# Rotary factors made in one go, a gain row spread by TensorE, and another order of products in the last MLP pieces

## The chip, the cores and the metric

One core of one Trainium2 chip runs the whole program. Its engines work side by side: TensorE (PE) multiplies matrices and transposes, VectorE (DVE) and ScalarE (ACT) work on tiles, GpSimd (POOL) does small operations and issues some DMAs, SyncE (SP) issues the others. Each engine takes its instructions in order and waits on semaphores for the others. The metric is the device time of one execution in microseconds (us); lower is better. The kernel before took 1451.28 us, the median of 3 runs (1450.83 to 1451.67).

## The reference

A two-layer encoder on 512 positions of width 1024, all in float32. Each layer is a token mixer and an MLP, each behind an RMS norm with a gain:

```python
for i in range(DEPTH):
    h = rms_norm(x, norm_mix[i])
    ...
    y = dilated_mixer(h, ...) if i == 0 else mla_mixer(h, ...)
    x = x + y
    h = rms_norm(x, norm_ffn[i])
    x = x + sq_relu_mlp(h, ffn_w1[i], ffn_w2[i])
```

The first mixer projects h to queries, keys and values of three head groups (eight heads of 128 each). Queries and keys of group g get an RMS norm per head with a gain of that group (`a_q_gain[g]`, `a_k_gain[g]`) and a rotary embedding:

```python
def rope(x, seq_len):
    ...
    return (xf * cos + rot * sin).astype(x.dtype)
def sq_relu_mlp(h, w1, w2):
    a = jax.nn.relu(h @ w1)
    return (a * a) @ w2
```

with w1 of 1024 x 4096 and w2 of 4096 x 1024.

## The kernel before

**Products.** Every float32 operand is split into a high and a low part (`whi` by ACT, `wlo` by DVE for weights; L220 and L221 for activations), and each product is three matmuls: high by high, high by low, low by high. The tile framework's scheduler puts the instructions of each engine in an order and inserts the waits, so the order on an engine is not that of the source.

**The start.** The tokens lie in four tiles of 128 x 1024. `load_x` (L249) loads a tile in two halves, `gain_table` (L223) loads a gain row and repeats it on all 128 partitions in the same DMA (512 KB written for 1024 numbers), `load_w0` (L253) loads the first four weight tiles of 512 KB, in turn with the token tiles. `norm_tile` (L206) squares a tile on ACT (L136), takes the root with a small DVE operation (L128) and a POOL operation (L131), multiplies by the root and the gain on DVE (L212), transposes on PE (L123) into a PSUM bank `tp` (two banks in all) and splits into `hT` (ACT L220, DVE L221). Weights in the first block are all loaded before its products run; these products write four `acc` banks (L184).

**The rotary tables.** `tables(g)` (L281) loads the two gain rows of group g, again one DMA each that repeats the row on all partitions, and multiplies them into the cosine and sine constants: four DVE operations of 128 x 512 (L289, L291), giving `cosg[g]` and `sing[g]`. It is called for group g when that group's first query and key block is about to be evacuated: DVE multiplies each `acc` bank by these tables (L308, L311). Groups 1 and 2 take the DMA target from a buffer of the evacuation (`t1`).

**The pool of gain tables.** `gp` holds one buffer of 128 x 1024 under the tag `gain`. Whoever takes the tag next waits until all readers of the one before are done.

**The MLP.** It is cut into four pieces of 1024 columns. `up` makes the first product, `down` calls `wino` (L489), which forms the second product by seven products of half-sized blocks instead of eight. `ORDER` (L590) names them: the product's number, the chain of PSUM banks it adds into (`a` is the pair `sc`, `b` the pair `tp`, `d` the pair `tp` or, in the last piece, two `acc` banks), whether it begins the chain, and where its sum goes. Each is 24 matmuls of 512 columns. Its activation operand is a block of the activations (products 1, 2 and 4) or a sum or difference of blocks, made by DVE (L517); `split_a` (L483) splits it into `asp`. Its weights lie in four slots of `wqs`; products 6 and 4 need a sum of weight blocks, which is made by a DMA issued from POOL that adds into the slot (L509, 512 KB, two for each product). Such a DMA waits until the slot's earlier weights are split (L523, L524). After each product `put` (L551) adds its banks into `resid` (DVE L554); in the last piece (`done` is given) a finished row tile goes on to the next norm.

**Between the layers.** The second mixer's own tables, `cgB` and `sgB`, are made on POOL: eight products (L691, L692) and a sign change (L693), from gains `gr` that SP loads (L684) once the buffer they go to is free. POOL has one queue for these and for the DMAs of L509.

Of the kernel before, what the change touches and what calls it, by code (L numbers as in the profile page):

```python
# [17 lines left out]
P = 128  # L18
# [69 lines left out]
def encoder_kernel(ctx: ExitStack, tc: tile.TileContext, x, norm_mix, norm_ffn, a_w_qkv, a_q_gain, a_k_gain,  # L88
# [6 lines left out]
    def nm(s):  # L95
        uid[0] += 1
        return f"{s}_{uid[0]}"
# [143 lines left out]
    with tc.tile_pool(name="apool", bufs=1, reuse_waits="tile") as ap_, \  # L241
# [7 lines left out]
        def load_x(r):  # L249
            for hf in range(2):  # L250
                nc.sync.dma_start(xts[r][:, 512 * hf:512 * hf + 512], x_v[:, r, 512 * hf:512 * hf + 512])
# [2 lines left out]
            early[("first", k)] = load_raw(*qk_units(0, 0)[k], 512)  # L254
        cas = ap_.tile([P, 2176], F32, name="ca")
        ca = cas[:, 0:C_ALL - C_KEEP]
        load_x(0)
        gain_b = gain_table(norm_mix[0:1, :].rearrange("o d -> (o d)"), D, "g_mix0")
        nc.sync.dma_start(ck[:, 0:P], consts[:, 0:P])
        load_w0(0)  # L260
        load_x(1)
# [6 lines left out]
        nc.sync.dma_start(ck[:, P:C_KEEP], consts[:, P:C_KEEP])  # L268
        for r in range(NT):
            norm_tile(r, xts[r], gain_b, hT, aw, xn_tag="qkT")  # L270
        gqk0 = ap_.tile([P, 2, 512], F32, tag="gqk", name="gqk")

        def cc(a, b):
            return ca[:, a - C_KEEP:b - C_KEEP]
# [4 lines left out]
        sel, r4, sel2, i4 = cc(C_SEL, C_R4), cc(C_R4, C_SEL2), cc(C_SEL2, C_I4), cc(C_I4, C_ALL)  # L279

        def tables(g):  # L281

            gqk = gqk0 if g == 0 else aw.tile([P, 4, DH], F32, tag="t1", name=nm("gq"))
            for t, src in enumerate((a_q_gain, a_k_gain)):
                nc.sync.dma_start(gqk[:, t, 0:DH], src[0, g].partition_broadcast(P))
            for t in range(2):
                gb = gqk[:, t, 0:DH].rearrange("p (f d) -> p f d", f=2).unsqueeze(1)
                gb = gb.broadcast_to([P, NT, 2, 64])
                V.tensor_tensor(cosg[g][:, :, t].rearrange("p r (f d) -> p r f d", f=2),  # L289
                                cosA.unsqueeze(2).broadcast_to([P, NT, 2, 64]), gb, op=ALU.mult)  # L290
                V.tensor_tensor(sing[g][:, :, t].rearrange("p r (f d) -> p r f d", f=2), sinA, gb, op=ALU.mult)  # L291
# [197 lines left out]
    def wino(tag, Aq, w, wqs, pool, resid, done=None):  # L489
# [66 lines left out]
                    done(2 * i + t, n)  # L556

        banks = {}
        for p, chain, first, (i, n, op) in ORDER:
            a, wq = operands(p)  # L560
            at = split_a(a, pool)
            if first:
                pl, tg = {"a": (sc_p, "sc"), "b": (tp_p, "tp"), "d": (tp_p, "tp")}[chain]
                if done is not None and chain == "d":
                    pl, tg = acc_p, "acc"
                banks[chain] = [pl.tile([P, 512], F32, tag=tg, name=nm(tg)) for _ in range(2)]
            bk = banks[chain]

            tail = done is not None and p in (7, 4)
            parts = {}  # L570
            for u, t in ((0, 0), (1, 0), (0, 1), (1, 1)) if tail else ((0, 0), (0, 1), (1, 0), (1, 1)):
                if u not in parts:
                    parts[u] = split_w(wq[u])
                hi, lo = parts[u]
                for j in range(2):
                    k = 2 * u + j
                    ah = at[:, k, 0, t * P:(t + 1) * P]
                    al = at[:, k, 1, t * P:(t + 1) * P]
                    for i_, (lt, rt) in enumerate(((ah, hi), (ah, lo), (al, hi))):
                        PE.matmul(bk[t], lhsT=lt, rhs=rt[:, j], start=(first and k == 0 and i_ == 0),  # L580
                                  stop=(k == 3 and i_ == 2), skip_group_check=True)
            put(i, n, op, bk)
# [3 lines left out]
    for _ in range(3):  # L586
# [3 lines left out]
    ORDER = [(1, "a", True, (0, 0, ALU.add)), (5, "b", True, (1, 1, ALU.add)), (3, "b", False, (0, 1, ALU.add)),  # L590
             (6, "a", False, (0, 1, ALU.subtract)), (2, "d", True, (0, 0, ALU.add)),
             (7, "a", False, (1, 1, ALU.subtract)), (4, "a", False, (1, 0, ALU.add))]

    def mlp(layer, w1, w2, hT_m, resid, pool, done):
        a2s = {}
# [352 lines left out]
```

## Time and profile before

| | us |
|---|---|
| median of 3 runs | 1451.28 |
| the profiled execution | 1451.78 |
| its span on the core | 1449.6 |
| PE busy | 1410.4 |
| DVE busy | 887.1 |
| ACT busy | 727.2 |
| POOL busy | 198.4 |
| waits of PE for the first normalised tile | 8.9 |

The profile is one execution, taken by the hardware. A row of its timeline gives the start in us from the span's beginning, the duration in us, the engine, the line of the kernel, the operation, what is written from what (with partitions x elements), how many instructions the row holds, and in brackets the idle time ahead of it with what ended it. A row of the waits gives the engine, the tile and line that waited, what it waited for, the sum in us, how many times and the longest. A row of the windows gives a stretch, its length, the busy time of PE, its weight loads (PEld), DVE, ACT and POOL with the number of instructions, the granted TensorE clock as a share of full speed, the DMA share and GB/s.

### The profile page before, as it was taken

How to read it: one execution, taken by the hardware profiler on the slowest of the kernel's cores; microseconds unless marked ns; L12 is line 12 of the kernel's file. 1: busy time of each engine (PE TensorE's matmuls, PEld its weight loads, DVE VectorE, ACT ScalarE, POOL GpSimd, SP SyncE). 2: the span in 40 equal slices, each digit the busy share in tenths (PEclk: the TensorE clock that was granted, in tenths of full speed). 3: DMA queues.
4: the chain of work that ended last, by engine and by line, in shares of the span. 5: the costliest groups of instructions: out<-in, count | busy, mean ns of one | idle time of the engine just before them, and what ended most of it. 6: DMA issues, size and time to landing. Idle time of an engine off the chain costs nothing.

```text
span 1449.6 us, 19315 instructions
## 1 busy us (share of the span) xinstructions
PE 1410.4 (97%) x7116; PEld 1196.8 (83%) x7116; DVE 887.1 (61%) x1421; ACT 727.2 (50%) x1590; POOL 198.4 (14%) x197
## 2 busy tenths in 40 slices
PE   7999999999999999999999999899999999999998
PEld 6889889889988878888888877776768988888877
DVE  6765566566537655266475749788755266475647
ACT  5544455355335533453544545777633454544543
POOL 1120120011011101011020222332101011020210
PEclk9999999999999999999999999999999999999999
DMA  7325114321622344749394853310013749394853
GB/s 228 100 57 162 58 49 129 110 63 45 174 92 62 97 140 141 222 112 236 91 233 127 195 136 66 99 30 30 30 44 136 206 111 239 93 223 138 189 116 88
DMA packets 134813, 177.52 MB, mean 122 GB/s; under 512 B 8768, under 2 KB 73536, under 8 KB 134720
## 3 DMA queue, kind: packets, MB, share of 16 engines
q1 hardware_dynamic: 117312, 142.74, 31.1%
q0 software_dynamic: 17408, 33.56, 14.0%
q8 instruction: 56, 0.92, 0.2%
q14 instruction: 37, 0.30, 0.1%
HBM read 172.07 MB, written 4.19 MB: 122 GB/s over the span
## 4 chain that ended last, share of the span: by engine, by line
PE 89%; ACT 4%; DVE 3%; DMA 2%; issue 1%; POOL 1%; SPq 0%; DVEq 0%; ACTq 0%; POOLq 0%
PE acc L184 58%; PE sc L580 10%; PE tp L580 7%; PE tp L123 4%; PE acc L859 1%; PE acc L835 1%; PE sc L753 1%; PE sco L444 1%; PE sco L440 1%; PE sc L351 1%; PE sc L835 1%; ACT whi L157 1%; ACT junkb L136 1%; DVE wlo L158 1%; PE tp L859 0%
## 5 line engine op out<-in xcount | busy, mean ns | idle before, releaser
L184 PE MATMUL acc<-whi,hT 128*128 128x512 f32 (+2 forms) x1600 | 486.3, 379 | 5.6 <-DVE t L311 2.2
L158 DVE TENSOR_TENSOR wlo<-raw,whi 128x1024 fp32r<-128x1024 f32 (+3 forms) x170 | 195.7, 1156 | 230.5 <-ACT whi L157 229.5
L184 PEld LDWEIGHTS acc<-whi,hT 128*128 128x128 f32 x1600 | 296.2, 189 | 47.3 <-issue 2.9
L184 PE MATMUL acc<-hT_f,whi 128*128 128x512 f32 (+1 forms) x1152 | 319.4, 366 | 1.9 <-DVE resid L641 1.2
L157 ACT ACTIVATE whi<-raw 128x1024 fp32r<-128x1024 f32 (+3 forms) x170 | 170.0, 1005 | 269.0 <-PE acc L184 177.4
L184 PE MATMUL acc<-wlo,hT 128*128 128x512 f32 (+2 forms) x800 | 300.2, 375 | 0.2 <-DVE wlo L158 0.2
L184 PEld LDWEIGHTS acc<-hT_f,whi 128*128 128x128 f32 x1152 | 208.4, 189 | 37.8 <-DVE resid L641 1.6
L524 DVE TENSOR_TENSOR wlo<-wqs,whi 128x1024 fp32r<-128x1024 f32 x112 | 137.3, 1227 | 113.6 <-ACT whi L523 113.5
L184 PE MATMUL acc<-hT_f,wlo 128*128 128x512 f32 (+1 forms) x576 | 205.1, 365 | 0.0
L523 ACT ACTIVATE whi<-wqs 128x1024 fp32r<-128x1024 f32 x112 | 118.6, 1060 | 167.6 <-PE acc L184 66.2
L184 PEld LDWEIGHTS acc<-wlo,hT 128*128 128x128 f32 x800 | 151.2, 189 | 20.5 <-DVE wlo L158 1.1
L580 PE MATMUL sc<-whi,asp 128*128 128x512 f32 x512 | 165.1, 390 | 0.8 <-ACT asp L485 0.8
L509 POOL DMA_DIRECT2D wqs<-in_ffn_w_dram x64 | 77.6, 1350 | 528.4 <-DVE wlo L524 339.9
L184 PEld LDWEIGHTS acc<-hT_f,wlo 128*128 128x128 f32 x576 | 108.6, 189 | 17.5
L131 POOL TENSOR_TENSOR qrs<-rs_v,nhalf 128x4 f32<-128x4 f32 x48 | 61.5, 1290 | 408.3 <-DVE rs_v L128 393.8
L580 PE MATMUL tp<-whi,asp 128*128 128x512 f32 x352 | 112.2, 390 | 2.6 <-DVE asp L486 2.6
L580 PEld LDWEIGHTS sc<-whi,asp 128*128 128x128 f32 x512 | 96.1, 188 | 21.6 <-ACT asp L485 1.6
L580 PE MATMUL sc<-wlo,asp 128*128 128x512 f32 x256 | 99.6, 389 | 0.0
L580 PEld LDWEIGHTS tp<-whi,asp 128*128 128x128 f32 x352 | 65.9, 188 | 17.2 <-DVE asp L486 3.5
L580 PE MATMUL tp<-wlo,asp 128*128 128x512 f32 x176 | 68.5, 389 | 0.0
L136 ACT ACTIVATE junk<-acc 128x128 f32<-128x128 f32 x192 | 53.1, 277 | 18.9 <-PE acc L184 13.8
L554 DVE TENSOR_TENSOR resid<-resid,sc 128x512 f32<-128x512 f32 x64 | 43.0, 682 | 24.4 <-PE sc L580 24.4
(190 smaller groups left out, 1796.3 us busy)
## 6 DMA issues: line engine op xcount, KB each, us to landing
wqs<-in_ffn_w_dram SPq DMA_DIRECT2D x80, 512.0 KB, 5.1
raw<-in_ffn_w_dram SPq DMA_DIRECT2D x64, 512.0 KB, 4.4
wqs<-in_ffn_w_dram POOLq DMA_DIRECT2D x64, 512.0 KB, 7.2
raw<-in_a_w_qkv_dram SPq DMA_DIRECT2D x96, 256.0 KB, 3.4
raw<-in_a_w_qkv_dram SPq DMA_DIRECT2D x64, 192.0 KB, 2.8
raw<-in_a_w_o_dram SPq DMA_DIRECT2D x8, 512.0 KB, 4.0
raw<-in_b_w_o_dram SPq DMA_DIRECT2D x8, 512.0 KB, 3.7
xt<-in_x_dram SPq DMA_DIRECT2D x8, 256.0 KB, 5.7
```

What stands on the lines that cost most here:

```text
L123: PE.transpose(o, i, ident)
L131: G.tensor_tensor(out, v[:, :n], nhalf[:, :n], op=ALU.pow)
L136: A.activation(junk, x, AF.Square, scale=1.0 / math.sqrt(dim), accum_out=out)
L157: A.activation(hi[:, :nk, :n], raw[:, :nk, :n], AF.Copy)
L158: V.tensor_tensor(lo[:, :nk, :n], raw[:, :nk, :n], hi[:, :nk, :n].bitcast(F32), op=ALU.subtract)
L184: PE.matmul(accs[o][:, oc], lhsT=lt, rhs=rt, start=(kt == 0 and p_i == 0 and hv == 0), stop=(kt == total - 1 and p_i == 2), skip_group_che ...
L509: nc.gpsimd.dma_start(t, src, accum_op=ALU.add)
L523: A.activation(hi, x, AF.Copy)
L524: V.tensor_tensor(lo, x, hi.bitcast(F32), op=ALU.subtract)
L554: V.tensor_tensor(sl, sl, banks[t], op=op)
L580: PE.matmul(bk[t], lhsT=lt, rhs=rt[:, j], start=(first and k == 0 and i_ == 0), stop=(k == 3 and i_ == 2), skip_group_check=True)
L835: PE.matmul(sc, lhsT=lt, rhs=rt, start=(i == 0), stop=(i == 4))
```

## The change

Three parts. First, the gain row of the first norm is loaded as one row of 4 KB, ahead of the tokens, and spread over the partitions by two PE products of a column of ones with it; ACT copies the two PSUM banks into the gain buffer. Second, the gain rows of all three groups are loaded at once, behind the first norms, into the buffer of the tag `gain` (so they wait for the last reader of the first norm's gain, and the next norm's gain waits for the last table), and `tables(g)` loads nothing. Third, the last piece of each MLP runs its products in the order 1, 2, 5, 3, 6, 7, 4 instead of 1, 5, 3, 6, 2, 7, 4.

```diff
+        gain_b = gp.tile([P, D], F32, tag="gain", name="g_mix0")
+        ones = ap_.tile([1, P], F32, tag="P10", name="ones")
+        V.memset(ones, 1.0)
+        row = ap_.tile([1, D], F32, tag="P01", name="g_row")
+        nc.sync.dma_start(row, norm_mix[0:1, :])
         load_x(0)
-        gain_b = gain_table(norm_mix[0:1, :].rearrange("o d -> (o d)"), D, "g_mix0")
+        for hf in range(2):
+            tp = tp_p.tile([P, 512], F32, tag="tp", name=nm("tpg"))
+            PE.matmul(tp, lhsT=ones, rhs=row[:, 512 * hf:512 * hf + 512], start=True, stop=True)
+            A.activation(gain_b[:, 512 * hf:512 * hf + 512], tp, AF.Copy)
         nc.sync.dma_start(ck[:, 0:P], consts[:, 0:P])
...
-        gqk0 = ap_.tile([P, 2, 512], F32, tag="gqk", name="gqk")
+        gqks = gp.tile([P, D], F32, tag="gain", name="gqk")[:, 0:2 * NG * DH].rearrange("p (g t d) -> p g t d", g=NG, t=2)
+        for g in range(NG):
+            for t, src in enumerate((a_q_gain, a_k_gain)):
+                nc.sync.dma_start(gqks[:, g, t], src[0, g].partition_broadcast(P))
...
         def tables(g):
-
-            gqk = gqk0 if g == 0 else aw.tile([P, 4, DH], F32, tag="t1", name=nm("gq"))
-            for t, src in enumerate((a_q_gain, a_k_gain)):
-                nc.sync.dma_start(gqk[:, t, 0:DH], src[0, g].partition_broadcast(P))
+            gqk = gqks[:, g]
...
-        for p, chain, first, (i, n, op) in ORDER:
+        for p, chain, first, (i, n, op) in ORDER if done is None else ORDER_LAST:
...
+    ORDER_LAST = [ORDER[0], ORDER[4]] + ORDER[1:4] + ORDER[5:]
```

The lines behind the first part move by 9 to 12, so L289 and L291 become L298 and L300, L308 and L311 become L317 and L320, L509 becomes L518, L580 becomes L589, L691 to L693 become L703 to L705.

The scheduler moves more than the diff shows. On DVE, behind the last normalisation of the first norm (`xn` of the fourth tile), there stood before, with tp numbered by its use (`tp_190` and `tp_197` of the third tile, `tp_212` and `tp_219` of the fourth):

```order
L212 SCALAR_TENSOR_TENSOR xn_205<-xt_113,nrs_209,g_mix_6_117 128x1024
L221 TENSOR_TENSOR hT_91<-tp_190,hT_91 128x4x128
L158 TENSOR_TENSOR wlo_263<-raw_259,whi_262 128x1024
L221 TENSOR_TENSOR hT_91<-tp_197,hT_91 128x4x128
L289 TENSOR_TENSOR cosg_104<-ca,gqk 128x4x128
L291 TENSOR_TENSOR sing_107<-ca,gqk 128x4x128
...
L221 TENSOR_TENSOR hT_91<-tp_212,hT_91 128x4x128
L221 TENSOR_TENSOR hT_91<-tp_219,hT_91 128x4x128
L308 TENSOR_TENSOR t_59_296<-acc_243,cosg_104 128x512
```

In the changed kernel (`tp_199` and `tp_206` are of the third tile, `tp_221` of the fourth; `cosg_105`, `cosg_106` are of groups 1 and 2) there stands:

```order
L212 SCALAR_TENSOR_TENSOR xn_214<-xt_113,nrs_218,g_mix_115 128x1024
L221 TENSOR_TENSOR hT_91<-tp_199,hT_91 128x4x128
L298 TENSOR_TENSOR cosg_104<-ca,gqk 128x4x128
L300 TENSOR_TENSOR sing_107<-ca,gqk 128x4x128
...
L300 TENSOR_TENSOR sing_108<-ca,gqk 128x4x128
L221 TENSOR_TENSOR hT_91<-tp_206,hT_91 128x4x128
L298 TENSOR_TENSOR cosg_106<-ca,gqk 128x4x128
L300 TENSOR_TENSOR sing_109<-ca,gqk 128x4x128
L317 TENSOR_TENSOR t_60_309<-acc_256,cosg_104 128x512
...
L221 TENSOR_TENSOR hT_91<-tp_221,hT_91 128x4x128
```

Eight table operations, for groups 0 and 1, now stand ahead of the low half of the third tile's second transposes, and four more, with an evacuation, ahead of the fourth tile's.

On ACT, in the first norm of the changed kernel, the second copy of the gain row (`tpg_125`) stands behind the first weight split, and the square of the fourth tile (`xn_214`) behind the fourth weight split (`whi_275`), which it stood ahead of before:

```order
L267 ACTIVATE g_mix_115<-tpg_122 128x512
L157 ACTIVATE whi_260<-raw_129 128x1024
L267 ACTIVATE g_mix_115<-tpg_125 128x512
...
L157 ACTIVATE whi_275<-raw_272 128x1024
L220 ACTIVATE hT_91<-tp_184 128x4x128
L136 ACTIVATE xn_214,nss_213<-xt_113 128x1024
```

The square of the fourth tile now waits for the landing of the fourth weights, since ACT takes its rows in order.

On POOL, at the end of the first MLP, the second layer's tables stood between the accumulating DMAs before; the last of the 29 in the first row is product 6's first, the row behind L692 its second:

```order
L509 DMA wqs_5335<-in_ffn_w_dram 128x2x512 x29
L691 TENSOR_TENSOR cgB<-ck,gr 128x4x32
L692 TENSOR_TENSOR sgB<-ck,gr 128x4x32
...
L509 DMA wqs_5335<-in_ffn_w_dram 128x2x512
L693 TENSOR_SCALAR sgB<-sgB 128x8x32
```

In the changed kernel all table operations stand ahead of product 6's two DMAs and product 4's two, the four of the last row:

```order
L518 DMA wqs_5342<-in_ffn_w_dram 128x2x512 x28
L703 TENSOR_TENSOR cgB<-ck,gr 128x4x32
L704 TENSOR_TENSOR sgB<-ck,gr 128x4x32
...
L705 TENSOR_SCALAR sgB<-sgB 128x8x32
L518 DMA wqs_5342<-in_ffn_w_dram 128x2x512 x4
```

Product 6's first DMA moved behind all nine table operations. On PE, two matmuls of product 6 (into `sc`) stand ahead of product 3's 24 (into `tp`, the operand `asp_7502`) in that piece, behind product 5 (`asp_7460`):

```order
L589 MATMUL tp_7464<-wlo_7482,asp_7460 128x512
L589 MATMUL tp_7464<-whi_7481,asp_7460 128x512
L589 MATMUL sc_7381<-whi_7544,asp_7541 128x512
L589 MATMUL sc_7382<-whi_7544,asp_7541 128x512
L589 MATMUL tp_7463<-whi_7505,asp_7502 128x512
```

Product 3 had two matmuls of product 6 ahead of it before too, when both came a product earlier; behind the first MLP's last piece the order on PE is that of before again, until the last piece of the second MLP, which is reordered in the same way.

More of the change, by code (lines that the diff above doesn't have):

```diff
@@ L281, in tables @@
         def tables(g):
-            gqk = gqk0 if g == 0 else aw.tile([P, 4, DH], F32, tag="t1", name=nm("gq"))
-            for t, src in enumerate((a_q_gain, a_k_gain)):
-                nc.sync.dma_start(gqk[:, t, 0:DH], src[0, g].partition_broadcast(P))
+            gqk = gqks[:, g]
             for t in range(2):
-                gb = gqk[:, t, 0:DH].rearrange("p (f d) -> p f d", f=2).unsqueeze(1)
+                gb = gqk[:, t].rearrange("p (f d) -> p f d", f=2).unsqueeze(1)
                 gb = gb.broadcast_to([P, NT, 2, 64])
```

## The prediction

> **What bounds the kernel now.** I read the page first, then what TensorE (PE) waited for, then the three stretches that the change touches.
>
> ```profile
> span 1449.6 us, 19315 instructions
> PE 1410.4 (97%) x7116; PEld 1196.8 (83%) x7116; DVE 887.1 (61%) x1421; ACT 727.2 (50%) x1590; POOL 198.4 (14%) x197
> ```
>
> ```profile
> PE tp L580 <- DVE asp L486: 2.6, 2, 1.5
> ...
> PE acc L184 <- DVE t L311: 2.2, 1, 2.2
> ...
> PE sc L580 <- ACT asp L485: 0.8, 2, 0.4
> ```
>
> PE is busy 97% of the span, so 1449.6 - 1410.4 = 39 us is all that can be won by waiting less. The last three rows (us in total, times, longest) are what the change aims at: 2.2 us in front of the rotary evacuation L311, 2.6 + 0.8 us in the second MLP products. The number of products is unchanged, so the whole question is which waits go and which come. Matmuls of 512 columns follow each other every 0.227 us, from the rows of the last MLP piece below: 24 of them from 860.05 to 865.49 are 5.44 us.
>
> **The change, part 1: the start and the rotary tables.** The rows are in order of time; the last column is the idle time before and its releaser.
>
> ```profile
> 4.51 1.06 ACT L136 ACTIVATE xn<-xt 128x1024 f32<-128x1024 f32 x1 [2.28 <-DMA xt<-in_x_dram]
> 7.53 1.29 DVE L212 SCALAR_TENSOR_TENSOR xn<-xt,nrs,g_mix 128x1024 f32<-128x1024 f32 x1 [1.68 <-DMA g_mix<-in_norm_mix_dram]
> 9.38 1.06 ACT L157 ACTIVATE whi<-raw 128x1024 fp32r<-128x1024 f32 x1 [3.72 <-DMA raw<-in_a_w_qkv_dram]
> 10.47 1.23 DVE L158 TENSOR_TENSOR wlo<-raw,whi 128x1024 fp32r<-128x1024 f32 x1 [1.65 <-ACT whi L157]
> 10.97 0.79 PE L184 MATMUL acc<-whi,hT 128*128 128x512 f32 x1
> 20.53 1.28 DVE L212 SCALAR_TENSOR_TENSOR xn<-xt,nrs,g_mix 128x1024 f32<-128x1024 f32 x1 [0.66 <-POOL nrs L131]
> 21.02 1.06 ACT L157 ACTIVATE whi<-raw 128x1024 fp32r<-128x1024 f32 x1 [0.37 <-DMA raw<-in_a_w_qkv_dram]
> 21.88 0.34 SPq L285 DMA_DIRECT2D gqk<-in_a_q_gain_dram  x1
> 26.39 0.69 DVE L289 TENSOR_TENSOR cosg<-ca,gqk 128x512 f32<-128x512 f32 x1 [1.82 <-DMA gqk<-in_a_q_gain_dram]
> 26.99 0.68 DVE L291 TENSOR_TENSOR sing<-ca,gqk 128x512 f32<-128x512 f32 x1
> 38.31 0.84 PE L184 MATMUL acc<-whi,hT 128*128 128x512 f32 x3
> ```
>
> Without the 512 KB broadcast all later loads land sooner. It held the first normalisation 1.68 us, and landed 3.0 us behind the first tile (4.51 to 7.53); I take 2.3 us, between the two. The spreading matmuls run while PE has nothing to do (its first instruction before stands at 8.87) and cost nothing by themselves. But ScalarE's second copy of the gain now stands behind the first weight split (1.06), and VectorE's first normalisation behind wlo (1.23): weights at 7.0, split to 8.1, wlo to 9.3, and from the normalisation's start to the first product 3.4 before (7.53 to 10.97), less the 0.5 in which ScalarE was then busy with the split: 12.2, over 1 us late. This does not add up with what follows, since a later chain takes over.
>
> That chain: ScalarE's fourth weight split now stands ahead of the fourth tile's square. Weights at 21.0 - 2.3 = 18.7, split 1.06, copy 0.6, square with its accumulator 1.25, the small operations and pow 0.9, normalisation 1.28: 23.8, against 20.53 + 1.28 = 21.81. The gain DMAs wait for it, since they use the buffer that it reads. They land 3.4 us after issue by the later gains' row (next part), 4.4 by the first group's (21.88 to 26.29, just before 26.39). The queue carries less then, so I take 3.4: tables start at T0 = 27.3. VectorE now does eight table operations, 0.60 apart (26.39, 26.99), before the low-half copy L221 for which PE's next transposes wait, and four more before that of the fourth tile: 8 x 0.60 + 0.60 (L221) + 1.2 (two tables) + 0.7 (L317 and a small one) + 1.2 (two tables) + 0.7 (L320) + 0.6 (L221) = 9.8, so 37.1. From the matmul that waits there, 22 more stand ahead of the first of the next block: 37.1 + 22 x 0.227 = 42.1. Before, that matmul was the second of the three in the row at 38.31, at 38.54. **Start: +3.6 us.** Bounds: 2.5 (the loads 1 us earlier still) and 4.6 (gains land in 4.4). Behind the gain DMAs on SP stand g_ffn, which waits for the last table, and the next weights; these need a buffer that the next block's first split frees, and that split stands behind the tables on VectorE, so the SP queue is not what they wait for.
>
> **Part 2: what the early tables give back.**
>
> ```profile
> DMA to landing us min/median/max: 3.4/3.7/3.9
> ```
>
> ```profile
> 88.02 0.69 DVE L289 TENSOR_TENSOR cosg<-ca,gq 128x512 f32<-128x512 f32 x1 [6.66 <-DMA gq<-in_a_q_gain_dram]
> 93.67 0.41 PE L184 MATMUL acc<-whi,hT 128*128 128x384 f32 x1 [2.24 <-DVE t L311]
> ```
>
> ```profile
> 95.02:98.44 3.42, 3.42 (x13) 3.42 (x12) 3.42 (x7) 1.08 (x5) 1.37 (x1) 0.50 0.61 171
> ...
> 523.60:525.80 2.20, 0.11 (x2) 0.05 (x1) 2.20 (x4) 1.06 (x1) 0.00 (x0) 1.00 0.01 4
> ```
>
> VectorE sat 6.66 us for the third group's gains, and PE then waited 2.24 us for the evacuations behind four tables. In the windows (length, busy time of PE, PEld, DVE, ACT, POOL, then the granted clock) 3.42 us at clock 0.50 follow: half of it, 1.71 us, is lost. With the tables made early both go, and what is late next, the weight splits at that place, had its data in time: **-3.95 us** (-2.2 if the slow stretch comes from elsewhere). Parts 1 and 2 together: **-0.3 us**.
>
> **Part 3: the last piece of the first MLP.**
>
> ```profile
> 860.05 0.39 PE L580 MATMUL sc<-whi,asp 128*128 128x512 f32 x1
> ...
> 865.49 0.39 PE L580 MATMUL tp<-whi,asp 128*128 128x512 f32 x1
> ...
> 868.06 0.73 PE L580 MATMUL tp<-whi,asp 128*128 128x512 f32 x2 [1.50 <-DVE asp L486]
> ```
>
> ```profile
> PE tp L123 <- DVE xn L212: 1.0, 1, 1.0
> ```
>
> ```profile
> 866.47 0.45 POOL L691 TENSOR_TENSOR cgB<-ck,gr 128x128 f32<-128x128 f32 x1
> ...
> 871.50 1.44 POOL L692 TENSOR_TENSOR sgB<-ck,gr 128x128 f32<-128x128 f32 x1
> ...
> 873.68 1.55 POOL L693 TENSOR_SCALAR sgB<-sgB 128x256 f32<-128x256 f32 x1
> ```
>
> ```profile
> 870.21 1.06 ACT L523 ACTIVATE whi<-wqs 128x1024 fp32r<-128x1024 f32 x1 [3.45 <-PE tp L580]
> ```
>
> ```profile
> DMA to landing us min/median/max: 6.2/6.4/7.9
> ```
>
> Product 2 takes its operand straight from the activations, so it needs none of the sums that product 5 waited for: the 1.50 us go, and with product 6 later also its 0.43. The next layer's norm can start a product earlier, which removes the 1.01 us at its first transposes (the row of that stretch's waits). Sum **-2.94 us** (0 at worst, were all of them to come back in another place).
>
> The price stands on POOL. Before, the first accumulating DMA of product 6 was issued ahead of the eight table operations of the second layer; now it stands behind all eight and L693. These wait for the gains gr, whose buffer the last matmuls ahead of product 1 free in both kernels; so they end at 871.50 + 1.44 + 1.55 = 874.5. The DMA lands 6.2 later (the quickest of four), at 880.7, and its split is done at 881.7. PE has 72 matmuls ahead (products 1, 2, 5): 860.05 + 72 x 0.227 = 876.4. Its next two are product 6's, and product 3's 24 stand behind them: **a stall of 5.4 us**. Bounds: 1.4 if four more tables take 0.45 like the third instead of 1.44; 7.1 if the landing takes 7.9. A stall of 2.24 us was followed by a slow stretch, so one of 5.4 should be too: **+1.7 us** (0 to 3.4). Part 3 is -2.94 + 5.4 + 1.7 = **+4.2 us**.
>
> By the Trainium skill, "TensorE: Matmul & The Clock Gate", "Why this matters for your kernels", only gaps of more than about 3 us between bursts cost the clock. By it the slow stretch after 2.24 us would not be owed to that gap, the sum of part 2 would be -2.2, and the new gap would still cost its 1.7, 1456.5 in all. The trace has a drop behind 2.24 us and none behind the gap in the window at 523.60, and the measurement decides. The Trainium skill, "DMA: Bandwidth & Descriptors", "Anatomy of one DMA — SWDGE (gpsimd) path", prices a POOL transfer at 2.0 us plus bytes over 436 GB/s, an estimate of 3.2 us for 512 KB; by it the stall would be 2.4. The trace's 6.2 to 7.9 are nearly twice that and stand.
>
> **Part 4: the last piece of the second MLP.**
>
> ```profile
> 1409.92 1.22 DVE L524 TENSOR_TENSOR wlo<-wqs,whi 128x1024 fp32r<-128x1024 f32 x1
> ...
> 1412.92 0.73 PE L580 MATMUL tp<-whi,asp 128*128 128x512 f32 x2 [1.14 <-DVE asp L486]
> ```
>
> No tables stand on POOL here. The same reorder removes 1.14 + 0.33 (what is left of the totals 2.6 and 0.8). Product 3's first matmuls then stand behind product 6's and wait for a VectorE difference in their turn; nothing shows its size, between 0 and about 1.1 (the wait of the same kind just removed); I take 1.0, since VectorE does the same work in the same time. Product 6's first DMA adds into the buffer that product 5's split has read, and product 5 is now third: its first wlo takes the place of the row at 1409.92, done at 1411.1. The DMA lands by 1417.3 to 1419.0, its split is done by 1420.1, 1.7 us or more ahead of PE: PE had done 28 of the 72 matmuls at 1411.8, where the 1.14 us began, and 44 more take it to 1421.8. (In the first MLP the same distance from the piece's start is near 866, ahead of POOL's 874.5.) **-0.4 us.**
>
> **Sum.** -0.3 + 4.2 - 0.4 = +3.5 us. The profiled execution took 1451.78 us (span 1449.6 and 2.2 around it), 0.5 above the median of the runs; the difference carries over: 1451.28 + 3.5 = **1454.8 us**.
>
> **The rivals.** (a) The stall comes but the clock holds, or POOL's tables run faster: part 3 is then +2.5 or less, the sum +1.8, 1453.1. For it: gaps of 2 us left the clock at 1.00; against it: 5.4 is far longer. (b) On the other side: POOL gives no stall. The DMA then must land by 876.4 - 1.06 = 875.3, so be issued by 869.1, 5.4 us ahead of my 874.5. This needs the nine POOL operations in 5 us instead of 10.5, as if all took the 0.45 that one or two did. Then only the gains are left: -0.3 - 2.9 - 0.4 = -3.6, 1447.7: faster. (c) The early tables cost more: two stalls of some 1.5 us near 33 and 37 us, close together, cost the clock there (+1.7), or the gains land in 4.4 (+1.0): 1455.8 to 1457.5. (d) The change does not do what it says, the wait at 91 us staying in another form: part 2 falls short by up to 3.95, 1458.7; against it, nothing there reads gains any more. (e) The slow stretch at 95 us is not owed to the gap ahead of it and stays: part 2 is -2.2, 1456.5; for it speaks the gap at 523.60 that cost no clock, against it that nothing else stood still there. This is what the Trainium skill's rule on the clock, cited above, would make of it.
>
> **Chances.** Forecast 43%, (a) 26%, (b) 12%, (c) 12%, (d) 3%, (e) 4%. A measurement of this kernel can tell about 0.2%, 2.9 us, from no change: below 1448.4 is faster, above 1454.2 slower. (b) gives faster 0.12; (a) and the lower third of the forecast's spread give the same, 0.40; the rest slower, 0.48. The range leaves out (b), (d) and the end of (c): 1450.0 to 1457.6.
>
> **What would show it.** In the profile after: a PE wait of about 5 us on the split L523's data near 876 us, with POOL's table rows ahead of the first accumulating DMA, and a window at clock 0.50 behind it; no gap near 91 us, no drop at 95; the first matmul of the second block near 42 us. If POOL issues that DMA before 869, or the wait near 876 is missing, part 3 is wrong and with it the sign.

## The result, and the profile after

| | before | changed |
|---|---|---|
| median of 5 runs on one chip | 1450.83 us (1449.58 to 1451.67) | 1458.44 us (1457.45 to 1459.02) |
| ratio, 95% interval | | 1.0052 (1.0038 to 1.0067) |
| profiled execution | 1451.78 us, span 1449.6, mean granted clock 0.999 | 1458.44 us, span 1456.2, clock 0.994 |

The kernel became 7.6 us slower. On a second chip the changed kernel took 1457.78 us beside 1451.74, ratio 1.0044 (1.0031 to 1.0056): 6.0 us. The forecast was +3.5 us: the side was right, the size about half. Three executions were disturbed and stand outside the medians and ranges given below: the profiled one of the kernel that keeps PE busy (3676.68 us, so no row of it is shown), one of the kernel with one load for two groups (1860.83) and one of the kernel before (2252.59).

The first lines of the page of the changed kernel, the span, and each engine's busy time with its count of instructions:

```profile
span 1456.2 us, 19315 instructions
...
PE 1417.7 (97%) x7120; PEld 1202.4 (83%) x7120; DVE 886.0 (61%) x1422; ACT 729.1 (50%) x1592; POOL 201.3 (14%) x197
```

PE's idle time is what it was (1456.2 - 1417.7 = 38.5 us, 39.2 before), and PE is busy 7.3 us longer. Of these, 3.74 us are the four instructions that spread the gain row, in time in which PE only waited before. From its first transposes on (at 8.87 us before, at 12.16 now) the same 7116 instructions took 1414.0 us instead of 1410.4, with 30.0 us of idle time instead of 30.2: the waits that went and those that came cancel there, and the rest is matmuls that ran slower in some stretches, as the granted clock says too. So two questions have to be kept apart: where PE waits, and where its clock drops.

What PE waited for in three stretches of the changed kernel (us in total, times, longest): 12 to 130 us, the last piece of the first MLP, and that of the second:

```profile
PE tp L123 <- DVE rs_v L128: 6.0, 1, 6.0
PE acc L184 <- DVE hT L221: 1.4, 1, 1.4
PE tp L123 <- DVE hT L221: 1.0, 2, 0.6
...
PE sc L589 <- ACT whi L532: 4.4, 1, 4.4
...
PE tp L589 <- DVE resid L563: 0.9, 1, 0.9
```

The first row is the wait for the first normalised tile, which ends at 12.16 us. No wait is left near 91 us, and none of the three old ones in the first MLP; a wait of 4.4 us on a weight split stands there instead. In the second MLP 1.47 us became 0.9.

The start, rows in order of time (start, length, then the idle time before it and its releaser):

```profile
2.38 3.74 PE L266 MATMUL tpg<-g_row,ones 1*128 1x512 f32 x4 [2.38 <-DMA g_row<-in_norm_mix_dram]
...
8.60 1.06 ACT L157 ACTIVATE whi<-raw 128x1024 fp32r<-128x1024 f32 x1 [1.94 <-DMA raw<-in_a_w_qkv_dram]
...
11.39 1.06 ACT L157 ACTIVATE whi<-raw 128x1024 fp32r<-128x1024 f32 x1 [0.22 <-DMA raw<-in_a_w_qkv_dram]
...
13.31 0.60 ACT L220 ACTIVATE hT<-tp 128x512 fp32r<-128x512 f32 x1 [0.86 <-PE tp L123]
...
13.96 0.80 PE L184 MATMUL acc<-whi,hT 128*128 128x512 f32 x1
...
20.15 1.06 ACT L157 ACTIVATE whi<-raw 128x1024 fp32r<-128x1024 f32 x1 [2.84 <-DMA raw<-in_a_w_qkv_dram]
...
23.79 1.28 DVE L212 SCALAR_TENSOR_TENSOR xn<-xt,nrs,g_mix 128x1024 f32<-128x1024 f32 x1 [0.66 <-POOL nrs L131]
...
25.10 0.34 SPq L283 DMA_DIRECT2D gqk<-in_a_q_gain_dram  x1
...
28.58 0.69 DVE L298 TENSOR_TENSOR cosg<-ca,gqk 128x512 f32<-128x512 f32 x1 [2.91 <-DMA gqk<-in_a_q_gain_dram]
...
37.75 0.68 DVE L221 TENSOR_TENSOR hT<-tp,hT 128x512 fp32r<-128x512 f32 x1
38.48 0.74 PE L184 MATMUL acc<-whi,hT 128*128 128x512 f32 x2 [1.36 <-DVE hT L221]
...
43.40 0.84 PE L184 MATMUL acc<-whi,hT 128*128 128x512 f32 x3
```

The first product of the second block is the second matmul of the last row: about 43.6 us, where 38.54 stood before.

POOL in the last piece of the first MLP, and the split and product that wait for its transfer:

```profile
865.66 0.64 POOL L703 TENSOR_TENSOR cgB<-ck,gr 128x128 f32<-128x128 f32 x1 [26.44 <-DMA gr<-in_b_q_gain_dram]
...
874.25 1.71 POOL L705 TENSOR_SCALAR sgB<-sgB 128x256 f32<-128x256 f32 x1
875.92 2.50 POOL L518 DMA_DIRECT2D wqs<-in_ffn_w_dram  x2
...
882.26 1.06 ACT L532 ACTIVATE whi<-wqs 128x1024 fp32r<-128x1024 f32 x1 [4.98 <-DMA wqs<-in_ffn_w_dram]
883.37 1.22 PE L589 MATMUL sc<-whi,asp 128*128 128x512 f32 x2 [4.37 <-ACT whi L532]
```

Windows of 3.41 us of the changed kernel (busy time of PE, PEld, DVE, ACT, POOL; then granted clock, DMA share, GB/s), each drop with the window ahead of it:

```profile
523.52:526.93 3.41, 1.32 (x11) 1.01 (x10) 3.39 (x4) 1.06 (x1) 0.00 (x0) 1.00 0.19 73
526.93:530.34 3.41, 3.41 (x18) 3.41 (x17) 1.30 (x2) 1.19 (x2) 0.00 (x0) 0.50 0.31 60
878.51:881.92 3.41, 0.49 (x3) 0.07 (x1) 3.26 (x4) 0.00 (x0) 0.00 (x0) 1.00 1.07 178
881.92:885.33 3.41, 1.96 (x5) 1.58 (x6) 1.98 (x3) 1.39 (x2) 0.46 (x1) 0.50 0.70 128
885.33:888.75 3.42, 3.42 (x10) 2.65 (x9) 2.11 (x2) 2.73 (x3) 1.42 (x2) 0.50 0.51 63
...
939.95:943.36 3.41, 1.40 (x10) 1.35 (x10) 2.20 (x10) 3.38 (x18) 1.94 (x4) 1.00 0.16 66
943.36:946.77 3.41, 3.41 (x14) 2.75 (x13) 2.58 (x12) 3.12 (x13) 2.34 (x4) 0.50 0.02 5
1117.44:1120.85 3.41, 1.58 (x12) 1.18 (x11) 3.13 (x6) 1.46 (x4) 0.20 (x1) 1.00 0.94 336
1120.85:1124.26 3.41, 3.41 (x19) 3.41 (x18) 2.34 (x3) 1.47 (x2) 0.34 (x1) 0.50 1.01 354
```

Five windows at clock 0.50, where the profile before had one, at 95.02. Two follow the new wait near 882 us; the other three, at 527, 943 and 1121 us, lie where the change touches nothing.

Setting the matmuls of the two profiles side by side, one by one, shows where the 6.6 us of span arise. How much later the changed kernel's PE is:

| behind | later by |
|---|---|
| first product of the second block (before: 38.5 us) | 5.1 us |
| the old wait at 91 us and its slow window (before: 130 us) | a steady 0.85 |
| the slow window at 527 us | 2.47 |
| the last piece of the first MLP | 6.3, then 5.7 |
| the slow windows at 943 and 1121 us | 6.15, 7.13 |
| the last piece of the second MLP | 6.64 |

### The profile page after: what moved, and what is told of

Read it like the earlier page. It is cut to its first block, busy times and chain, and to the rows that moved or that the text cites. A ratio compares the mean times of both kernels' runs of the same rounds, so it can differ in the third digit from the quotient of the medians.

```text
span 1456.2 us, 19315 instructions
## 1 busy us (share of the span) xinstructions
PE 1417.7 (97%) x7120; PEld 1202.4 (83%) x7120; DVE 886.0 (61%) x1422; ACT 729.1 (50%) x1592; POOL 201.3 (14%) x197
## 4 chain that ended last, share of the span: by engine, by line
PE 86%; issue 3%; DVE 3%; ACT 3%; DMA 3%; POOL 1%; SPq 0%; ACTq 0%; POOLq 0%; DVEq 0%
PE acc L184 55%; PE sc L589 10%; PE tp L589 7%; PE tp L123 4%; PE acc L871 1%; DMA raw<-in_a_w_qkv_dram 1%; PE sc L765 1%; DMA wqs<-in_ffn_w_dram 1%; PE acc L847 1%; PE sco L449 1%; PE sco L453 1%; PE sc L360 1%; DVE wlo L158 1%; PE sc L847 1%; ACT junkb L136 1%
## 5 line engine op out<-in xcount | busy, mean ns | idle before, releaser
L532 ACT ACTIVATE whi<-wqs 128x1024 fp32r<-128x1024 f32 x112 | 118.8, 1060 | 166.8 <-PE acc L184 66.2
L589 PE MATMUL sc<-whi,asp 128*128 128x512 f32 x512 | 165.6, 391 | 4.5 <-ACT whi L532 4.4
L518 POOL DMA_DIRECT2D wqs<-in_ffn_w_dram x64 | 77.7, 1357 | 514.5 <-DVE wlo L533 333.1
L589 PEld LDWEIGHTS sc<-whi,asp 128*128 128x128 f32 x512 | 96.2, 188 | 25.6 <-ACT whi L532 4.8
L589 PE MATMUL tp<-whi,asp 128*128 128x512 f32 x352 | 113.6, 394 | 0.9 <-DVE resid L563 0.9
L589 PE MATMUL sc<-wlo,asp 128*128 128x512 f32 x256 | 99.6, 389 | 0.0
L589 PEld LDWEIGHTS tp<-whi,asp 128*128 128x128 f32 x352 | 67.1, 191 | 15.5 <-DVE resid L563 1.3
L589 PE MATMUL tp<-wlo,asp 128*128 128x512 f32 x176 | 68.9, 393 | 0.0
```

What stands on the lines that cost most here:

```text
L518: nc.gpsimd.dma_start(t, src, accum_op=ALU.add)
L532: A.activation(hi, x, AF.Copy)
```

## Experiments

The numbers on the steps are those of the prediction. All are timed in five rounds beside the kernel before on the same chip; a median stands with the lowest and highest run, a ratio with its 95% interval. The first four ran on one chip, the next four on a second, then three on a third and one on a fourth.

### The order alone

```diff
+    ORDER_LAST = [ORDER[0], ORDER[4]] + ORDER[1:4] + ORDER[5:]
-        for p, chain, first, (i, n, op) in ORDER:
+        for p, chain, first, (i, n, op) in ORDER if done is None else ORDER_LAST:
```

> Only the new order of products in the last MLP pieces; start and rotary tables as before. Theory A (POOL's table operations hold up product 6's accumulating DMA): a PE wait of 4 to 5.5 us in the first MLP's last piece with one or two windows at half clock behind it, against 2.9 + 0.4 us of removed waits: +3 to +5 us against before, 1454 to 1456. Theory C (the extra half-clock stretches of the changed kernel belong to its start and come with it): +3 us at most and no half-clock stretch besides the one at 95 us and those behind the long wait. Theory B (the order itself is bad, whatever POOL does): cannot be told from A here, see e3.

Measured: 1455.06 us (1452.66 to 1456.76), ratio 1.0021 (1.0012 to 1.0030), +3.3. PE's wait and the POOL rows of this kernel:

```profile
PE sc L580 <- ACT whi L523: 4.3, 1, 4.3
```

```profile
872.09 1.71 POOL L696 TENSOR_SCALAR sgB<-sgB 128x256 f32<-128x256 f32 x1
873.76 2.50 POOL L509 DMA_DIRECT2D wqs<-in_ffn_w_dram  x2
```

The wait comes with the reorder alone, and its first DMA stands behind the last table here too. Two windows at 0.50 follow it, from 879.94 us; two others stand at 94.88 and 1118.88 us.

### The start alone

The changed kernel with the old order in both MLPs:

```diff
-        for p, chain, first, (i, n, op) in ORDER if done is None else ORDER_LAST:
+        for p, chain, first, (i, n, op) in ORDER:
```

> Only the spread gain row and the early rotary tables; the order of products as before. Theory A: the start loses 4.9 us and the removed wait at 91 us with its half clock gives back 3.95: +1.0 us, 1452, with a chance of plus or minus one half-clock stretch (1.7 us), since the gaps of some 2 us near 524, 940 and 1118 us lose clock only where they fall within one window of the clock. Theory C: the same +1.0 and the extra half-clock stretches at 527, 943 and 1121 us in nearly every run: +3.8 us, 1455.

Measured: 1453.61 us (1451.10 to 1455.00), ratio 1.0011 (1.0002 to 1.0020), +1.9, more than theory A's +1.0 and less than theory C's +3.8. The wait at 91 us is gone and the old waits of the first MLP (1.5, 0.7, 0.4) are back. Its profiled execution has no slow window at all. So the start costs time by itself, and the two halves add to 1.9 + 3.3 = 5.2 us by medians, against 7.6 and 6.0 for the whole.

### POOL's tables in three operations

```diff
-            for t in range(2):
-                for hf in range(2):
-                    gb = gr[:, t, hf * 32:hf * 32 + 32].unsqueeze(1).broadcast_to([P, NT, 32])
-                    G.tensor_tensor(cgB[:, :, t, hf * 32:hf * 32 + 32], cosB, gb, op=ALU.mult)
-                    G.tensor_tensor(sgB[:, :, t, hf * 32:hf * 32 + 32], sinB, gb, op=ALU.mult)
+            gb = gr.rearrange("p t (f d) -> p (t f) d", f=2).unsqueeze(1).broadcast_to([P, NT, 4, 32])
+            for tab, cs in ((cgB, cosB), (sgB, sinB)):
+                G.tensor_tensor(tab.rearrange("p r t (f d) -> p r (t f) d", f=2),
+                                cs.unsqueeze(2).broadcast_to([P, NT, 4, 32]), gb, op=ALU.mult)
```

> The changed kernel with the second layer's tables made by 3 POOL operations (two of 128x512 and the sign) instead of 9. Theory A: POOL is done with them 6 to 8 us sooner, product 6's DMA is issued near 867 instead of 876, the PE wait of 4.4 us and the half clock behind it (2.7 us) go: 6 to 7 us faster than the changed kernel, near 1451.5. Theory B: the wait stays, near 1458.

Measured: 1454.89 us (1453.52 to 1456.48), ratio 1.0020 (1.0010 to 1.0030), about 3 us below the changed kernel. POOL's rows, and PE's waits in that piece:

```profile
864.64 2.15 POOL L702 TENSOR_TENSOR cgB<-ck,gr 128x512 f32<-128x512 f32 x1 [27.15 <-DMA gr<-in_b_k_gain_dram]
866.74 2.27 POOL L702 TENSOR_TENSOR sgB<-ck,gr 128x512 f32<-128x512 f32 x1
869.11 1.71 POOL L704 TENSOR_SCALAR sgB<-sgB 128x256 f32<-128x256 f32 x1
870.79 1.26 POOL L518 DMA_DIRECT2D wqs<-in_ffn_w_dram  x1
```

```profile
PE tp L589 <- DVE resid L563: 1.5, 1, 1.5
PE sc L589 <- ACT whi L532: 0.9, 1, 0.9
```

The DMA is issued 5.1 us sooner (870.79 for 875.92), and the wait on its split shrinks by 3.5, from 4.4 to 0.9 us. That settles the place of the stall: POOL's queue. Theory A had twice the gain, 6 to 7 us: a new wait of 1.5 us on a bank that VectorE frees came in place of the old one (the first row of the waits), and this profile still has slow windows at 880.56, 938.59 and 1116.08 us.

### The kernel before, unchanged

> The kernel before, unchanged, for the clock of each run. Theory A (the clock's windows run free of the program): the same median within 0.1%, but the mean granted clock differs from run to run by 0.001 to 0.003, the time goes with it by about 1.7 us for each 0.0012, and this profile's half-clock stretches stand behind other gaps than the one at 91 us alone. Theory C: one half-clock stretch, at 95 us, in each run.

Measured: 1451.79 us (1449.18 to 1454.09), ratio 1.0001 (0.9993 to 1.0010). Its profiled execution took 1453.68 us at a granted clock of 0.995; windows of it, in the same columns:

```profile
91.92:95.33 3.41, 1.56 (x9) 1.59 (x10) 3.41 (x8) 0.92 (x4) 0.00 (x0) 1.00 0.69 197
522.00:525.41 3.41, 1.32 (x12) 1.20 (x12) 3.41 (x5) 1.56 (x2) 0.00 (x0) 1.00 0.01 2
525.41:528.82 3.41, 3.41 (x19) 3.41 (x18) 0.48 (x1) 0.69 (x2) 0.00 (x0) 0.50 0.50 147
931.60:935.01 3.41, 1.94 (x10) 0.93 (x8) 1.99 (x7) 3.38 (x15) 1.53 (x3) 1.00 0.62 186
935.01:938.42 3.41, 2.74 (x10) 2.67 (x11) 2.73 (x12) 2.92 (x16) 2.25 (x5) 0.50 0.02 5
1112.50:1115.92 3.42, 1.75 (x13) 1.55 (x14) 2.76 (x6) 1.75 (x3) 0.55 (x1) 1.00 0.98 352
1115.92:1119.33 3.41, 3.41 (x19) 3.41 (x18) 2.39 (x3) 1.32 (x2) 0.00 (x0) 0.50 1.03 360
```

The same program that dropped once, at 95 us, drops here at 525, 935 and 1116 us (a second window follows the one at 935), and not at 95, although it still waits 2.3 us there. The drops at 527, 943 and 1121 us of the changed kernel therefore need no cause in the change. Over the four chips the runs of this kernel spread with the clock: mean 1449.7 us at a granted clock of 1.000 (17 runs), 1451.4 at 0.999 (42), 1453.0 at 0.996 (20), 1454.3 at 0.995 (6); between them, at 0.998 and 0.997, 1452.5 (11) and 1452.0 (8). So 0.005 of clock went with 4.6 us, and not with the 7 that theory A's rate makes of it.

### The changed kernel again

> The changed kernel, unchanged, beside the others on one chip. Theory A: its waits are those of its first profile (4.4 us in the first MLP, none at 91 us), but the half-clock stretches near 527, 943 and 1121 us come in some runs and not in others; median about 5 us (start 1.7 by e2 plus order 3.3 by e1) above before rather than 7.6, since five runs are few for a chance of 1.7 us each; clock 0.993 to 0.998. Theory D (the parts disturb each other): 7.6 again, with both parts together dearer than the sum.

Measured: 1457.78 us (1457.06 to 1458.26), as given above. The profile has slow windows at 525.74, 880.72 (two), 942.16 and 1119.65 us: the same five places as in the first profile, which theory A did not expect; the time lies between the two theories. All ten runs of the changed kernel had clocks from 0.993 to 0.996.

### The gain row alone, and the tables alone

The first is the kernel before with the row load, the two spreading products and the two copies, and nothing else of the change; the second is the kernel before with all gains loaded behind the first norms, and the old gain broadcast.

> Only the gain row spread by TensorE; tables loaded and made group by group as before. Theory A (the loads land only 0.9 us sooner, and the first normalisation waits behind the first weight split): first product of the first block 3 us late, the first of the second block 1 to 2 us late, the wait at 91 us and its chance of a half-clock stretch as before: +1 to +2 us. Rival (the early tables alone delay the start): within 0.5 us of before.

> Only the tables of all groups made behind the first norms, the gain row loaded as before. Theory A: the gains are issued near 22 as before, eight table operations more on VectorE ahead of the fourth tile's low half: the first product of the second block 2 to 3 us late, the wait at 91 us gone: -1 to +1 us against before. Rival (the spread row alone delays the start): the second block on time, and the whole 2.2 us or more gained.

Measured: the row alone 1454.80 us (1452.10 to 1457.31), ratio 1.0018 (1.0009 to 1.0028), +3.1 (theory A had +1 to +2), with the second block's first product at 42.8 us, 4.3 late. Two groups of transposes that stood behind that product stand ahead of it there; set side by side one by one, PE's instructions are a steady 3.3 us late from 60 us on. The tables alone 1452.06 us (1451.53 to 1455.62), ratio 1.0006 (0.9997 to 1.0015), not told apart from no change; the second block starts on time, at 38.44. There the wait at 91 us did not go, it changed its form:

```profile
91.83 0.84 ACT L157 ACTIVATE whi<-raw 128x768 fp32r<-128x768 f32 x1
...
92.71 0.96 DVE L158 TENSOR_TENSOR wlo<-raw,whi 128x768 fp32r<-128x768 f32 x1 [3.97 <-ACT whi L157]
...
95.08 0.66 PE L184 MATMUL acc<-whi,hT 128*128 128x384 f32 x1 [3.28 <-DVE rs_v L128]
```

The weight split now stands behind the softmax rows on ScalarE, VectorE sits 3.97 us for it, and PE goes on only at 95.08, behind the evacuations. So the row by itself makes most of the start's loss, 4.3 of the 5.1 us. The early tables by themselves neither cost nor gain a measurable amount in this form, though they stand ahead of the third and fourth tiles' L221 there too: their first starts at 26.18 us there. The rest of the loss comes only with both parts, when the first table starts at 28.58 us and PE waits 1.36 us behind the tables.

### Groups 1 and 2 loaded together, nothing else

The kernel before, with the gains of the second and third group put into one buffer near 50 us, so that the third group's tables need not wait at 88 us for a load:

```diff
+            if g == 1:
+                gq12.append(aw.tile([P, 4, DH], F32, tag="t1", name=nm("gq")))
+            gqk = gqk0 if g == 0 else gq12[0][:, 2 * g - 2:2 * g]
+            for gg in ((0,), (1, 2), ())[g]:
+                dst = gqk0 if gg == 0 else gq12[0][:, 2 * gg - 2:2 * gg]
```

> Another way to the same end: kernel before, but the gains of groups 1 and 2 are loaded together when group 1's buffer is free (near 50 us), so the start is as before and nothing waits near 88 us. Theory A: -2.2 us for certain and up to -3.9 where the old gap cost clock; the first block unchanged, 1448 to 1449.5. Rival (the wait at 91 us is hidden anyway, or comes back in another form): within 1 us of before.

Measured: 1449.91 us (1446.20 to 1450.55), ratio 0.998 (0.997 to 0.999): the only kernel so far that beats the one before. PE waits for nothing between 12 and 120 us. At a granted clock of 1.000 its two runs average 1446.3 us, 3.4 below the 1449.7 of the kernel before; at 0.996 its six runs average 1450.3, 2.8 below. That is the 2.24 us of the wait, and 0.5 to 1.2 that no row here explains.

### PE kept busy in the new gap

The changed kernel with 20 products with a matrix of zeros, added to the accumulators at the place where PE waits; nothing is left out.

```diff
+            if done is not None and tag == 3 and p == 5:
+                zt = pool.tile([P, P], F32R, tag="zt", name="zt", bufs=1)
+                A.activation(zt, ck[:, 0:P], AF.Copy, scale=0.0)
+                for d in range(20):
+                    PE.matmul(banks["a"][d % 2], lhsT=zt, rhs=at[:, d % 4].rearrange("p s c -> p (s c)"),
+                              start=False, stop=False, skip_group_check=True)
```

> The changed kernel with 20 products of a zero matrix (4.5 us of PE work that adds zeros to product 6's banks) ahead of product 6 in the first MLP's last piece, so PE works through the wait for the DMA. Theory A (the two windows at half clock behind the wait belong to PE's idleness in it): no wait of 4.4 us, no half clock near 882, 2 to 3 us faster than the changed kernel, near 1455. Rival (the half clock has another cause there): the half clock stays, same time or slower than the changed kernel.

Measured: 1454.85 us (1453.57 to 1456.69), ratio 1.0022 (1.0013 to 1.0032), mean granted clock 0.998 where the changed kernel has 0.994. The products add work and take nothing away, and by its distance from the kernel before (+3.4 for +6.0 and +7.6) the kernel is some 3 to 4 us faster than without them, with the higher clock. That they spare just the two slow windows behind the gap fits the forecast, but is not shown, since no row of its profile tells it.

### The gain row copied by VectorE

```diff
-            A.activation(gain_b[:, 512 * hf:512 * hf + 512], tp, AF.Copy)
+            V.tensor_copy(gain_b[:, 512 * hf:512 * hf + 512], tp)
```

on the row-alone kernel. This was to undo the first loss at the start, the second copy behind the first weight split.

> As e6 (gain row spread by TensorE, nothing else), but VectorE copies both halves, so no copy stands behind ACT's first weight split and the first normalisation stands ahead of VectorE's first wlo. Theory A (e6's loss is the place of the second copy and of the normalisation in the queues): the first product near 10 to 11 instead of 13.4, e6's loss of 2.5 us shrinks to 0 to 1.5 us against before. Rival (the loss is the square of the fourth tile behind the fourth weight split, or the loads): as e6, +2 to +3 us.

Measured: 1454.36 us (1452.38 to 1457.24), ratio 1.0020 (1.0011 to 1.0028): no better than the row with ScalarE's copies. My theory fell. Rows of its start:

```profile
6.88 1.29 DVE L212 SCALAR_TENSOR_TENSOR xn<-xt,nrs,g_mix 128x1024 f32<-128x1024 f32 x1
...
11.48 1.06 ACT L157 ACTIVATE whi<-raw 128x1024 fp32r<-128x1024 f32 x1 [0.34 <-DMA raw<-in_a_w_qkv_dram]
...
12.45 1.06 ACT L220 ACTIVATE hT<-tp 128x512 fp32r<-128x512 f32 x2
...
13.08 0.79 PE L184 MATMUL acc<-whi,hT 128*128 128x512 f32 x1 [2.89 <-ACT hT L220]
```

The first normalisation is 0.65 us earlier than before the change (6.88 for 7.53), yet the first product is 2.1 us later (13.08 for 10.97): the copies hT that it needs stand on ScalarE behind the second weight split, which waits for its data until 11.48. Before, they stood ahead of it. The gains are issued at 25.21, as in the changed kernel. PE's last wait in the first 45 us of this kernel ends at 15.65 us (1.35 us, on L221), so the late square of the fourth tile, the rival's reason, costs nothing here. By these rows the loss lies in the order that the row gives to ScalarE's work, not in who copies it; a kernel with the row and the old ScalarE order was not tried, so no run shows it.

### Two combinations

The one load for two groups, with the row copied by VectorE; and the one load with a different last piece, in which product 2 stands third, ahead of the tables' place in POOL's queue:

```diff
+    ORDER_LAST = ORDER[0:2] + [ORDER[4]] + ORDER[2:4] + ORDER[5:]
```

> e8 (gains of groups 1 and 2 in one load) with the row spread as in e10. Theory A: e8's -2 to -3 us plus what e10 shows against before; only if e10 is at or below before is this faster than e8. Rival (they do not add): as e8.

> e8 (one load for the gains of groups 1 and 2) with the products of the last pieces in the order 1, 5, 2, 3, 6, 7, 4: product 2 early, but product 5 still second, so product 6's first DMA keeps its place ahead of POOL's table operations. Theory A (the price of the change's order is that DMA's place behind the tables): no wait of 4 us in the first MLP, 0.4 to 1.4 us of small waits gone there and in the second MLP: 0 to 2 us faster than e8, so -2 to -5 us against before. Theory B (product 2 early costs by itself, through VectorE or the banks): slower than e8, by 1 us or more.

Measured: the first 1452.43 us (1449.86 to 1452.88), ratio 1.0006 (0.9998 to 1.0015), 1.0 us above the kernel before beside it. The one load alone lies 1.8 us below, the row copied by VectorE 2.9 above: the two add, as theory A has it, and the row costs there too. The second 1449.62 us (1446.51 to 1452.44), ratio 0.9987 (0.9978 to 0.9995). Its POOL rows, then PE's waits in the first and the second MLP:

```profile
855.30 1.20 POOL L515 DMA_DIRECT2D wqs<-in_ffn_w_dram  x1 [20.56 <-DVE wlo L530]
861.93 1.26 POOL L698 TENSOR_TENSOR cgB<-ck,gr 128x128 f32<-128x128 f32 x1 [5.43 <-DMA gr<-in_b_q_gain_dram]
```

```profile
PE sc L586 <- DVE resid L560: 2.8, 1, 2.8
...
PE sc L586 <- DVE resid L560: 2.3, 1, 2.3
```

The DMA goes out at 855.30, ahead of all tables, and the wait of 4.4 us is gone. But products 6 and 7 now follow each other in the same banks, and PE waits 2.8 and 2.3 us until VectorE has emptied them, so the small waits of theory A's sum were not gained. Its ratio and that of the one load alone, 0.9987 and 0.998, lie within each other's intervals. Both beat the kernel before and the changed one; the one load alone is the smaller edit.

## Why the prediction was right or wrong

**The side was right, and for its reason.** The wait on the split L532 came at 4.4 us (forecast 5.4), behind a first accumulating DMA issued at 875.9 (forecast 874.5); the order alone reproduces it and shorter POOL work removes most of it. The three old waits of that piece went, -2.94 us as forecast. The 2.24 us at 91 us went. The second MLP gave -0.5 us (1.47 to 0.9; forecast -0.4), though the new waiter needs a bank that VectorE's addition frees, not a difference.

**Step that failed: part 1, "Without the 512 KB broadcast all later loads land sooner ... I take 2.3 us".** Taking the broadcast off the queue let the fourth weights' split start 0.9 us sooner (20.15 for 21.02), and the first weights' 0.8 (8.60 for 9.38); 18.7 was forecast for the fourth. The last normalisation ended at 25.07 instead of 23.8, and the tables started at 28.58 instead of 27.3. The rest of that chain held: 3.4 us from issue to landing, then 9.85 us from the first table to the end of the last L221 (9.8 forecast). So the start cost 5.1 us instead of 3.6. The error was to read one wait that the broadcast ended (1.68 us) as time that all later loads would win. The upper bound of 4.6 missed too: it let the gains land late, but not the weights. The first product came at 13.96, not 12.2, which, as forecast, this later chain covers.

**Step that failed: part 3, "a slow stretch ... +1.7 us".** The clock cost two windows, not one. In the first, from 881.92, PE was still idle 1.45 us (3.41 - 1.96), and the next stayed at 0.50. They cost 0.98 (half of the 1.96 busy) and 1.71 us, 2.7 together. The terms of this part come to -2.94 + 4.4 + 2.7 = +4.2, the forecast's own number by two errors that cancel; by position the piece cost 3.3 to 3.8.

**Step that failed: the clock as owed to the length of a gap.** Parts 2 and 3 booked -1.71 us for the slow window at 95 and +1.7 for the new one, so the clock came to nothing. Without any clock the measured terms are 5.1 - 2.24 - 2.94 + 4.4 - 0.5 = **+3.8 us**, near the forecast +3.5. The clock made the rest: 2.2 to 3.8 us, taking 6.0 and 7.6 for the whole. The profile after agrees: PE was busy 3.6 us longer for the same instructions. Runs of equal clock agree: at 0.995 and 0.996 the three runs of the changed kernel average 1457.6 us and those of the kernel before 1453.3, 4.2 us apart. So do the halves: the order alone is 1.0 us above the kernel before at a clock of 0.995 (1455.3 for 1454.3; its terms are -2.94 + 4.4 - 0.5 = +1.0), the start alone 2.4 at 1.000 (1452.0 for 1449.7; its terms 5.1 - 2.24 = +2.9). The unchanged kernel has the drop at 95 in one profile and not in another, so the -1.71 was never sure, and the two windows at 882, which no profile of the old order has, were a cost beyond the forecast. A drop followed where enough of a gap fell into one window of the clock, not where a gap was long (last section).

**Rivals.** (a) fell with the clock, which did not hold. (b), no stall, is refuted. The reasons of (c) did not come: the gains landed in 3.4 us, and the waits of 0.61 and 1.36 us that end at 34.14 and 38.48 us cost no clock. Of (e), the slow window at 95 not owed to the gap alone, half is right: the gap is needed, its place decides. The gap at 523.60 that cost no clock shows it: an edge at 525.10 us cut it, so that 1.44 us of idle time fell into one window; in the second profile of the same kernel 2.09 fell into the window at 522.00, and the next was slow. (d) did happen, but only with the tables alone; with the row the second block is late, and the changed kernel has no wait there.

**Open.** The order alone and the start alone add to 5.2 us, the whole is 6.0 to 7.6. The halves' intervals add to 1.0014 to 1.0050, those of the whole begin at 1.0031 and 1.0038, so the halves may well add. The changed kernel's slow windows at 527, 943 and 1121 us, in both of its profiles, cost by position some 2.5 to 3 us. That both its profiles have them, and that none of its ten runs had a clock above 0.996 where most runs of the kernel before lie higher, may be an effect of where the new gap and the late start put the program, or chance; no run here tells.

## What to carry to other kernels

POOL, which both computes and issues transfers, does so in one queue here (the transfer went out at 875.92 us, behind nine table operations): before a step is moved, look what then stands ahead of its DMA in such a queue, and add the landing time. A wait of about 2 us can cost 1.7 us more by the clock in one execution and nothing in the next, so a change of a few us is judged by many runs, and at equal granted clock. Try the smallest edit that removes the wait: one early load for two groups gained some 2 us, where the change that also moved two other things lost 6 to 8.

## What the runs showed of the hardware

The slow windows stand on a grid. In the profile after they start at 526.93, 881.92, 943.36 and 1120.85 us: 104, 122 and 174 times 3.4133 us behind the first. In a new execution the grid lies elsewhere against the program. What counts is how long PE is idle inside one window, such as 1.83 us at 1117.44 (3.41 less 1.58) or 2.01 at 939.95. Cut from 25 us on by the grid that their own slow windows give, the profiles of this case, all but that of the kernel that keeps PE busy, 13 in number, have 3463 windows at full clock. Of those with 1.9 us or more of idle time all 21 were followed by one at 0.50, of those with 1.6 to 1.9 us 9 of 14, and of the rest only one (1.47 us, at 931.60 of the unchanged kernel). The 2.3 us wait of the unchanged kernel was cut by an edge, so that 1.85 fell into one window (91.92), and no drop followed. Inside a slow window less is enough: all five with 0.67 us or more of idle time (1.45 at 881.92) were followed by a second at 0.50, and none of the 31 with 0.51 or less. The Trainium skill, "TensorE: Matmul & The Clock Gate", "What's actually happening", says that the window is free-running and 3413 ns long; the multiples above agree. The same page, "Why this matters for your kernels", puts drops behind gaps of more than about 3 us; here waits near 2 us sufficed when they fell into one window, and the measurement decides.

POOL's table operations of 128x128 took 0.46 or 1.44 us within one piece, and two of 128x512 took 2.15 and 2.27: four times the elements in one operation cost less than two of the slow small ones.
